# A running sum of squares: additions on GpSimd replaced by accumulating DMAs between SBUF tiles

## The chip, the core and the metric

One NeuronCore of a Trainium2 chip. The metric is the device time of one execution in microseconds; lower is better.

## The reference

The program computes two blocks on 512 tokens of 1024 features, in float32. The first is a recurrent layer (RG-LRU) with a layer norm, then a mixture of 32 experts with a second layer norm. The second block, where the change lies, has two layers, each of three parts with an RMS norm ahead of each, and an RMS norm at the very end:

```python
def rmsnorm(x, g):
    xf = x.astype(jnp.float32)
    y = xf * lax.rsqrt(jnp.mean(xf * xf, axis=-1, keepdims=True) + EPS)
    return (y * g.astype(jnp.float32)).astype(x.dtype)
...
    for l in range(DEPTH_2):
        h = rmsnorm(x, g_ffn1[l])
        x = x + 0.5 * swiglu(h, w1_a[l], w3_a[l], w2_a[l])
        h = rmsnorm(x, g_mix[l])
        p = h @ w_in[l]
        ...
        x = x + merged @ w_o[l]
        h = rmsnorm(x, g_ffn2[l])
        x = x + 0.5 * swiglu(h, w1_b[l], w3_b[l], w2_b[l])
    return rmsnorm(x, g_final)
```

So there are seven norms: three ahead of each layer's parts, twice, and the last one. The mixer in the middle of a layer has gates, a Fourier branch, a short convolution and a pooling branch; only its end and its place matter here.

## The kernel before

The dense stage keeps x transposed: `X[k]`, k = 0 to 7, holds features 128k to 128k + 127 on the partitions and all 512 tokens along the row, in float32. Weights stream in from DRAM in blocks of 1 MB; each half block (128 x 1024) is split into a high part `whi` (ScalarE, L135) and a low part `wlo` (VectorE, L136). Every product of a 128 x 128 weight tile is three matmuls of 128 x 512 (L172 to L174): high by high, high by low, low by high.

A norm needs, for each token, the sum of x squared over all 1024 features, that is over the partitions of eight tiles. The kernel adds up the squares tile by tile into `ssum` (128 x 512), and then sums over the partitions with TensorE: `rstd_1` multiplies pieces of `ssum` by a vector of ones (L1230), and VectorE and ScalarE make the factor 1/sqrt from it. The factor is not needed ahead of the next matmuls: those run on X times the gain (`xgh`, `xgl`, made by `prep`, L1218 and L1224), and their results are multiplied by the factor `R` afterwards.

How the pieces are laid in time:

- The second half of an FFN (`out_part`) goes through j = 0 to 7; for each j it sums ten products into one bank (30 matmuls), then `done(j)` adds the bank to `X[j]` on VectorE (L1342) and calls `nxt(j)`, which is `prep`: the high part on ScalarE, then `square(j)`, and the low part on VectorE.
- The second half of a mixer (`out_part2`) does the same with four products for each j, the fourth one three steps later. Towards its end only fourth products are left, so the last `done(j)` follow each other quickly (L1486).
- `square(k)` squares `X[k]` on ScalarE (L1208) into a buffer `t`, one of seven; for k = 0 it writes `ssum` itself. The addition of `t` to `ssum` (L1211) is put on a list, `late`, that is emitted after the next square by `flush`. Its engine is the argument `E`, GpSimd by default. Only the first of the seven norms passes VectorE (`squares`, called as `pre` of the first FFN).
- Behind the first two chunks of the next part (24 matmuls each) stands `rstd_1`, in TensorE's queue; in the very first FFN it is behind three. The engines take their instructions in the order in which they are emitted. Waits between engines, and those for DMAs, come from the tiles that instructions read and write.
- The last norm has its squares for k = 0 to 6 in `last`, which also scales the odd `X[k]` on GpSimd (L1495). The last tile, k = 7, is done by `tail` in two halves of 256 tokens, where `sums` (L1516) reads `ssum` and the squares of the last tile, with half of the second half's matmuls behind it.

GpSimd has, in the dense stage, these additions, L1495's scalings, some small memsets for the convolution's and the pooling's edges (L1355, L1356, L1424, L1425) and, at the very end, multiplications for the output (L1537). SyncE issues all weight loads.

Of the kernel before, what the change touches and what calls it, by code (L numbers as in the profile page):

```python
# [16 lines left out]
OP = mybir.AluOpType  # L17
# [12 lines left out]
CAP = 64  # L30
# [34 lines left out]


class Stream:
    """Weight blocks of 128 x 2048 in the order of use: DMA, then each half as hi + lo."""

    def __init__(self, tc, wpool, nr, nh):  # L70
        self.tc, self.nc = tc, tc.nc
# [9 lines left out]
        self.ns = 0  # L81

    def slots_from(self, pool, tag, n, lo=0, hi=1 << 30, bufs=None):
        """n more raw buffers, for blocks lo to hi"""
        new = [dict(pool=pool, tag=tag, bufs=bufs or n, blk=None, lo=lo, hi=hi) for _ in range(n)]
        self.slots += new
        return new

    def add(self, aps, keep=()):
        """keep: blocks that are not split but read as they come"""  # L90
        self.blocks += aps
        self.keep = set(keep)
        self.used = set()
# [44 lines left out]
        return True  # L138

    def split_first(self, i):  # L140
        """A piece of the first half"""
        a, b = FIRST[i]
        hi, lo = (t[:, a:b] for t in self.get(0))
        src = self.raw[0][:, a:b]
        self.nc.scalar.activation(hi, src, AF.Copy)
        self.nc.vector.tensor_tensor(lo, src, hi, op=OP.subtract)
# [5 lines left out]
        return self.half[h]  # L152

    def advance(self, h, defer=False):
        """Everything of half h (and before) has been emitted. defer: returns the low parts still to be emitted"""
        late = []
        self.used |= {b for b in self.keep if 2 * b + 1 <= h}
        while self.ns < min(2 * len(self.blocks), self.hold):
            ahead = sum(q // 2 not in self.keep for q in range(h + 1, self.ns + 1))
            if ahead > self.nh - 1 or self.ns // 2 >= self.nb + 1:  # L160
                break
            self._dma()
            if self.ns // 2 >= self.nb:
                break
            self._split(late if defer else None)
        self._dma()
        return late
# [120 lines left out]
def rec_phase(K):  # L288
# [253 lines left out]
        nc.gpsimd.tensor_tensor(x1l[c], zz[c], x1h[c], op=OP.subtract)  # L542

    PSW = {}
    # the first of two token tiles is ahead of the second at the end
    steps = [(k, i) for k in range(KR - 3) for i in range(2)]
    steps += [(KR - 3, 0), (KR - 2, 0), (KR - 3, 1), (KR - 1, 0), (KR - 2, 1), (KR - 1, 1)]

# [32 lines left out]
        nc.gpsimd.dma_start(t, A["ln1"][i:i + 1].to_broadcast([128, D]))  # L581
    for c in range(2, 4):
        PSW[c] = [bank() for _ in range(2)]
    # the first of the two further ahead
    steps = [(k, i) for k in range(4) for i in range(2)]
    steps += [(4, 0), (5, 0), (4, 1), (6, 0), (7, 0), (5, 1), (8, 0), (9, 0), (6, 1), (7, 1), (8, 1), (9, 1)]
    late = {1: [(ln_s, 0)], 3: [(ln_a, 1)], 5: [(ln_s, 1), (logits_t, 0), (ln_b, 0)],
# [37 lines left out]


def onehot(K, g, cs=range(4)):
    """One-hot rows of the slots of 4 experts: token on the partitions, slot on the columns"""
    nc, op, io = K["tc"].nc, K["op"], K["io"]
    V, P = nc.vector, nc.gpsimd if g else nc.vector  # L630
    if ("oh", g) not in K:
        K["oh", g] = (op.tile([128, 4, 4 * CAP], F32R, name="oh", tag="oh", bufs=2),
                      op.tile([128, 4, 2], F32, name="sg", tag="sg", bufs=2))
        P.tensor_scalar(K["oh", g][1], K["slot"], float(-4 * CAP * g), None, op0=OP.add)
    oh, sg = K["oh", g]
    for c in cs:
        if g and c < 3:
            for i in range(2):
                P.tensor_scalar(oh[:, c + i], io, sg[:, c, i:i + 1], None, op0=OP.is_equal)
            P.tensor_tensor(oh[:, c], oh[:, c], oh[:, c + 1], op=OP.add)  # L640
        else:
            V.tensor_scalar(oh[:, c], io, sg[:, c, 0:1], None, op0=OP.is_equal)
            V.scalar_tensor_tensor(oh[:, c], io, sg[:, c, 1:2], oh[:, c], op0=OP.is_equal, op1=OP.add)
# [66 lines left out]


def route_ids(K):
    """The ids of the tokens by expert"""
    pm, ohm = K["pm"], K["ohm"]
    P = K["tc"].nc.gpsimd
    bm = [128, 4, 2, NE]
    K["dd"] = K["gp"].tile([128, 4, NE], F32R, name="dd")
    P.tensor_tensor(pm, ohm, K["tid"][:, :, :, None].to_broadcast(bm), op=OP.mult)
    P.tensor_tensor(K["dd"], pm[:, :, 0], pm[:, :, 1], op=OP.add)
# [18 lines left out]
def moe_phase(K):  # L738
# [61 lines left out]
    HP, HS, YP = {}, {}, {}  # L800

    def mm_h(e, m, i):
        """Half of the features of the product of expert e with w1 or w3: columns 0:64 x high, 64:128 x low"""
        nonlocal h
        name = ("h1", "h3")[m]
        if i == 0:
            HP[m] = bank(name)
        ps = HP[m]
        for q in range(2):
            w = st.get(h)  # L810
            for r in range(2):
                k = 4 * i + 2 * q + r
                if e == 0 and m == 0:
                    if k == 0:
                        gather(0, 0)
                    if k + 1 < KD:
                        gather(0, k + 1)
                x = XT[e // 4][k][:, e % 4]
                sl = slice(r * 512, (r + 1) * 512)
                if k < KD - 1:  # L820
                    nc.tensor.matmul(ps, x, w[0][:, sl], start=k == 0, stop=False)  # L821
                nc.tensor.matmul(ps[:64], x[:, 0:64], w[1][:, sl], start=False, stop=False)  # L822
                if k == KD - 1:
                    nc.tensor.matmul(ps, x, w[0][:, sl], start=False, stop=True)  # L824
            if i and q:
                HS[m] = mp.tile([128, 512], F32, name=name + "s", tag=name + "s", bufs=1)
                act(HS[m], ps, AF.Copy)
            st.advance(h)
            h += 1
# [42 lines left out]
                in_=ysb, in_offset=None, bounds_check=2 * S - 1, oob_is_err=False)  # L872

    def place(c):
        """For the last two experts: gate by token and slot"""
        oh, sg = K["oh", NE // 4 - 1]
        if c == 0:
            K["og"] = (mp.tile([128, 4, 128], F32, name="og", tag="og", bufs=1), mp.tile([128, 128], F32, name="og1"))
        og, o1 = K["og"]
        for k, o in ((0, og[:, c]), (1, o1)):  # L880
            nc.gpsimd.tensor_scalar(o, io[:, 128:256], sg[:, c, k:k + 1], K["gt"][:, c, k:k + 1], op0=OP.is_equal, op1=OP.mult)
        nc.gpsimd.tensor_tensor(og[:, c], og[:, c], o1, op=OP.add)

    def place_t():
        """The same with the slot on the partitions"""
        P = mp.tile([128, 4, 128], F32, name="P", tag="P", bufs=1)
        pt = bank("ids")
        for c in range(4):
            nc.tensor.transpose(pt[:, c * 128:(c + 1) * 128], K["og"][0][:, c], ident)
        act(P, pt.rearrange("p (c t) -> p c t", c=4), AF.Copy)  # L890
        return P

    def overflow(nmax):
        """Slots beyond CAP of an expert, 64 at a time, for any routing."""
        NI = 16
        m7 = mp.tile([128, NE, 8], F32, name="ova", tag="og", bufs=1)
        xe = mp.tile([128, 2, NE], F32, name="xe")
# [169 lines left out]
        return [bank(*n) for n in ((("h1",), ("h3",)), (("y0",), ("y1",)), (("gat", 2), ("gat", 2)), (("ht",), ("ids",)))[c]]  # L1067

    def comb(c, *ab):
        """Sums of products into the two halves of z or of what has yet to be added to it"""  # L1070
        new = c not in PC
        if new:
            PC[c] = banks(c)
# [2 lines left out]
                nc.tensor.matmul(PC[c][i], a, b[:, i * 512:(i + 1) * 512], start=new and n == 0, stop=n == len(ab) - 1)  # L1076

    def stats(c):
        """z complete, its mean and variance"""
        m = mv[:, c]  # L1080
        for i in range(2):
            z = PC[c][i]
# [57 lines left out]


def both(f, g):
    """The steps of two sequences in turn"""
    f, g = iter(f), iter(g)
    go = True
    while go:
# [6 lines left out]


def newton(V, out, v, t):
    """The steps to out = 1/sqrt(v) from t = sqrt(v), one Newton step"""
    yield lambda: V.reciprocal(out, t)
    yield lambda: V.tensor_tensor(t, out, out, op=OP.mult)
    yield lambda: V.tensor_tensor(t, t, v, op=OP.mult)
# [4 lines left out]
def dense_phase(K):  # L1164
# [41 lines left out]
    def square(k, E=nc.gpsimd):  # L1206
        t = ssum if k == 0 else tmp()
        act(t, X[k], AF.Square)  # L1208
        flush()
        if k:  # L1210
            late.append(lambda: E.tensor_tensor(ssum, ssum, t, op=OP.add))  # L1211

    def prep(k, g, sq=True):
# [10 lines left out]
        late.insert(0, lambda: STT(lo, X[k], g(k), hi, op0=OP.mult, op1=OP.subtract))  # L1224

    def rstd_1():
        """rc = 1/sqrt(mean of squares + eps), a token on a partition"""
        pc = bank()
        for c in range(4):
            nc.tensor.matmul(pc[:, 2 * c:2 * c + 2], ssum[:, c * 128:(c + 1) * 128], onesf[:, 0:2],  # L1230
# [6 lines left out]
        TT(rc[:, 3], rc[:, 0], rc[:, 0], op=OP.mult)  # L1237

    def rstd_2(*out):
        """rc or its square, a token a column"""  # L1240
        for i in out:
            ps = bank()
            for c in range(4):
# [15 lines left out]
        return ps  # L1259

    def out_part(x, done, tail=None):
        """X[j] += x @ w for every j, the tiles of w in the order (j, k). tail: takes the last j instead"""
        nonlocal h
        n = 0
        for j in range(KD):
# [17 lines left out]
        h += n // 8  # L1283

    def out_part2(x, done):
        """The same for four x, the last one of them LAG2 j later"""
        nonlocal h
        ps = {}
        n = 0
# [19 lines left out]
    def ffn(nxt, pre=None, tail=None):  # L1309
        n = 0  # L1310

        def in_r():
            """A chunk, and behind an early one the steps to R"""
            nonlocal n
            ps = in_chunk()
            if n == 1 and pre:
# [178 lines left out]
            nc.gpsimd.tensor_scalar(X[k], X[k], vc("gfinal", k), None, op0=OP.mult)  # L1495

    def tail(x, w):
        """The last feature tile of X, the final norm and the output, half of the tokens ahead of the other half"""
        PX, PR = [bank() for _ in range(2)], {}
        sq = tmp()  # L1500

# [73 lines left out]


def layout(I):
    """The inputs as the program reads them: slices, transposes and zero padding only."""
    f = np.float32
    A = {}  # L1580
    x = np.asarray(I["x"])[0]
# [19 lines left out]
    A["ln1"] = np.ascontiguousarray(np.stack([np.asarray(I["ln_g"])[0, 0], np.asarray(I["ln_b"])[0, 0]]))  # L1601

    def tiles(w):
        """[K, N] -> [N/128, 128, K/128, 128]: for each chunk of outputs its stationary tiles."""
        K, N = w.shape
        return w.reshape(K // 128, 128, N // 128, 128).transpose(2, 1, 0, 3)

    blocks = []

    def put(a):  # L1610
        """[n, 128, 1024] halves"""
        a = np.asarray(a).reshape(-1, 128, HB)
        if len(a) % 2:
            a = np.concatenate([a, np.zeros((1, 128, HB), f)])
# [106 lines left out]
```

## Time and profile before

| | us |
|---|---|
| median of 2 runs | 3045.65 (3044.44 to 3046.87) |
| span of the profiled execution | 3045.3 |
| TensorE busy | 2972.5 (98%) |
| VectorE busy | 1743.2 (57%) |
| ScalarE busy | 1302.1 (43%) |
| GpSimd busy | 282.3 (9%) |

The profile is that of one execution of 3045.3 us from its first to its last instruction; the runs' median is 0.35 us above that. Shares are of the span. Matmuls overlap each other in TensorE, so that a busy share of 98% says that it hardly ever stands still, not that it is at its peak. The mean granted clock of TensorE is 0.991 of full speed.

### The profile page before, as it was taken

How to read it: one execution, taken by the hardware profiler on the slowest of the kernel's cores; microseconds unless marked ns; L12 is line 12 of the kernel's file. 1: busy time of each engine (PE TensorE's matmuls, PEld its weight loads, DVE VectorE, ACT ScalarE, POOL GpSimd, SP SyncE). 2: the span in 40 equal slices, each digit the busy share in tenths (PEclk: the TensorE clock that was granted, in tenths of full speed). 3: DMA queues.
4: the chain of work that ended last, by engine and by line, in shares of the span. 5: the costliest groups of instructions: out<-in, count | busy, mean ns of one | idle time of the engine just before them, and what ended most of it. 6: DMA issues, size and time to landing. Idle time of an engine off the chain costs nothing.

```text
span 3045.3 us, 33566 instructions
## 1 busy us (share of the span) xinstructions
PE 2972.5 (98%) x13360; PEld 2338.3 (77%) x13360; DVE 1743.2 (57%) x2127; ACT 1302.1 (43%) x1687; POOL 282.3 (9%) x235
## 2 busy tenths in 40 slices
PE   9997999999899999999999999999999999999998
PEld 7875666666568888888878888888888888878887
DVE  7678888898974344455555334443344465544343
ACT  4746888888753223233233223322223332332222
POOL 0025222220600000000010000100001000100002
PEclk9998999999999999999999999999999999999999
DMA  6374899999822222222222222222222222232221
GB/s 191 119 277 171 342 363 347 373 371 374 319 80 88 96 97 97 92 81 105 97 97 97 97 97 83 97 97 96 99 83 97 83 97 100 94 109 86 96 97 56
DMA packets 75360, 452.18 MB, mean 148 GB/s; under 512 B 8684, under 2 KB 19308, under 8 KB 22336
## 3 DMA queue, kind: packets, MB, share of 16 engines
q1 hardware_dynamic: 71040, 441.78, 39.4%
q0 software_dynamic: 3072, 7.17, 0.6%
q8 instruction: 106, 1.74, 0.2%
q10 hardware_dynamic: 1088, 1.05, 0.1%
q14 instruction: 54, 0.44, 0.0%
HBM read 439.79 MB, written 14.16 MB: 149 GB/s over the span
## 4 chain that ended last, share of the span: by engine, by line
PE 77%; DVE 4%; ACT 2%; issue 1%; POOL 0%; POOLq 0%; DVEq 0%; ACTq 0%
PE mm L172 23%; PE mm L173 23%; PE mm L174 23%; DVE wlo L136 2%; PE y L857 2%; PE h L822 2%; PE h L821 1%; ACT whi L135 1%; PE ht L835 1%; PE gat L792 1%; DVE xgl L1224 0%; DVE z L1064 0%; DVE X L1486 0%; PE h L824 0%; ACT X L1114 0%
## 5 line engine op out<-in xcount | busy, mean ns | idle before, releaser
L136 DVE TENSOR_TENSOR wlo<-raw,whi 128x1024 fp32r<-128x1024 f32 x533 | 663.9, 1255 | 432.3 <-ACT whi L135 432.3
L172 PE MATMUL mm<-xgh,whi 128*128 128x512 f32 x2048 | 810.6, 396 | 2.2 <-ACT xgh L1218 2.2
L173 PE MATMUL mm<-xgl,whi 128*128 128x512 f32 x2048 | 809.8, 395 | 2.1 <-DVE xgl L1224 2.1
L174 PE MATMUL mm<-xgh,wlo 128*128 128x512 f32 x2048 | 809.2, 395 | 0.0
L135 ACT ACTIVATE whi<-raw 128x1024 fp32r<-128x1024 f32 x535 | 557.9, 1052 | 498.3 <-PE mm L173 457.3
L173 PEld LDWEIGHTS mm<-xgl,whi 128*128 128x128 f32 x2048 | 386.1, 189 | 94.5 <-DVE xgl L1224 4.3
L172 PEld LDWEIGHTS mm<-xgh,whi 128*128 128x128 f32 x2048 | 386.2, 189 | 93.1 <-ACT xgh L1218 2.6
L174 PEld LDWEIGHTS mm<-xgh,wlo 128*128 128x128 f32 x2048 | 386.1, 189 | 90.7
L172 PE MATMUL mm<-s,whi 128*128 128x512 f32 (+1 forms) x938 | 368.0, 392 | 0.0
L173 PE MATMUL mm<-s,whi 128*128 128x512 f32 (+1 forms) x938 | 367.9, 392 | 0.0
L174 PE MATMUL mm<-s,wlo 128*128 128x512 f32 (+1 forms) x938 | 367.8, 392 | 0.0
L1187 ACT ACTIVATE s<-t 128x512 fp32r<-128x512 f32 x128 | 81.0, 633 | 376.2 <-DVE t L1337 298.8
L1211 POOL TENSOR_TENSOR ssum<-ssum,t 128x512 f32<-128x512 f32 x41 | 57.0, 1391 | 1740.2 <-ACT t L1208 1739.5
L136 DVE TENSOR_TENSOR wlo<-rawb,whi 128x1024 fp32r<-128x1024 f32 x162 | 203.6, 1298 | 22.7 <-ACT whi L135 20.6
L172 PEld LDWEIGHTS mm<-s,whi 128*128 128x128 f32 x938 | 176.6, 188 | 40.8
L173 PEld LDWEIGHTS mm<-s,whi 128*128 128x128 f32 x938 | 176.6, 188 | 40.8
L174 PEld LDWEIGHTS mm<-s,wlo 128*128 128x128 f32 x938 | 176.6, 188 | 40.6
L822 PE MATMUL h<-wlo,xt 128*64 128x512 f32 x512 | 195.6, 402 | 7.0 <-DVE wlo L136 6.3
L1336 DVE TENSOR_TENSOR t<-mm,R 128x512 f32<-128x512 f32 x88 | 60.8, 691 | 224.4 <-PE mm L174 224.4
L821 PE MATMUL h<-whi,xt 128*128 128x512 f32 x448 | 181.4, 405 | 5.9 <-PEq L1033 5.0
L1342 DVE SCALAR_TENSOR_TENSOR X<-mm,X 128x512 f32<-128x512 f32 x63 | 43.6, 692 | 227.8 <-PE mm L174 227.8
L857 PE MATMUL y<-whi,hd 128*64 128x512 f32 x512 | 161.6, 397 | 2.5 <-ACT whi L135 1.5
(356 smaller groups left out, 3281.7 us busy)
## 6 DMA issues: line engine op xcount, KB each, us to landing
raw<-in_wblocks SPq DMA_DIRECT2D x265, 1024.0 KB, 4.8
rawb<-in_wblocks SPq DMA_DIRECT2D x81, 1024.0 KB, 6.8
rawa<-in_wblocks SPq DMA_DIRECT2D x57, 1024.0 KB, 6.6
YD<-cs SPq DMA_DIRECT2D x8, 512.0 KB, 7.3
xt<-in_wblocks SPq DMA_DIRECT2D x4, 1024.0 KB, 8.3
rawb<-YD SPq DMA_DIRECT2D x3, 1024.0 KB, 4.8
z<-in_x POOLq DMA_DIRECT2D x4, 512.0 KB, 9.3
raw<-in_dfts SPq DMA_DIRECT2D x2, 1024.0 KB, 4.8
```

Source lines behind the costliest of these rows:

```text
L135: self.nc.scalar.activation(hi, src, AF.Copy)
L136: f = lambda E=self.nc.vector: E.tensor_tensor(lo, src, hi, op=OP.subtract)
L172: nc.tensor.matmul(ps, wh, xh, start=first, stop=False)
L173: nc.tensor.matmul(ps, wh, xl, start=False, stop=False)
L174: nc.tensor.matmul(ps, wl, xh, start=False, stop=last)
L821: nc.tensor.matmul(ps, x, w[0][:, sl], start=k == 0, stop=False)
L822: nc.tensor.matmul(ps[:64], x[:, 0:64], w[1][:, sl], start=False, stop=False)
L857: nc.tensor.matmul(ps[i][:64], hd[:, f, v:v + 64], w[wv][:, sl], start=f == 0 and n == 0, stop=f == 3 and n == 2)
L1187: act(hi, src, AF.Copy)
L1211: late.append(lambda: E.tensor_tensor(ssum, ssum, t, op=OP.add))
L1336: TT(v, p3, R, op=OP.mult)
L1342: STT(X[j], ps, 0.5, X[j], op0=OP.mult, op1=OP.add)
```

## The change

In `square`, an addition whose engine is GpSimd becomes a DMA issued from GpSimd, which adds the tile `t` to `ssum` as it writes (`accum_op`). The additions of the first norm, which pass VectorE, stay. The other lines of the diff take out docstrings and comments.

```diff
@@ -1207,7 +1207,9 @@
         t = ssum if k == 0 else tmp()
         act(t, X[k], AF.Square)
         flush()
-        if k:
+        if k and E is nc.gpsimd:
+            late.append(lambda: nc.gpsimd.dma_start(ssum, t, accum_op=OP.add))
+        elif k:
             late.append(lambda: E.tensor_tensor(ssum, ssum, t, op=OP.add))
```

## Rows read from the trace of the kernel before

**Rows 1.** The page, parts 1 and 4: busy time by engine; shares of the chain.

```profile
PE 2972.5 (98%) x13360; PEld 2338.3 (77%) x13360; DVE 1743.2 (57%) x2127; ACT 1302.1 (43%) x1687; POOL 282.3 (9%) x235
...
PE 77%; DVE 4%; ACT 2%; issue 1%; POOL 0%; POOLq 0%; DVEq 0%; ACTq 0%
```

**Rows 2.** Instructions of line L1211: count; ns min/median/max, first and last start.

```profile
L1211 POOL TENSOR_TENSOR ssum<-ssum,t x41: 1291/1306/1661, 1197.1 to 3026.3; 128x512 f32<-128x512 f32 x41
```

**Rows 3.** Timeline of GpSimd behind an FFN: start, duration, instruction, [idle before <-releaser].

```profile
1197.12 1.30 POOL L1211 TENSOR_TENSOR ssum<-ssum,t 128x512 f32<-128x512 f32 x1 [345.55 <-ACT t L1208]
...
1239.01 1.30 POOL L1211 TENSOR_TENSOR ssum<-ssum,t 128x512 f32<-128x512 f32 x1 [5.68 <-ACT t L1208]
```

**Rows 4.** Timeline of TensorE: the reads of the sum in three norms.

```profile
1247.84 0.95 PE L1230 MATMUL mm<-onesf,ssum 128*128 128x2 f32 x8
...
1590.46 0.95 PE L1230 MATMUL mm<-onesf,ssum 128*128 128x2 f32 x8
...
3029.91 0.28 PE L1516 MATMUL mm<-onesf,ssum 128*128 128x2 f32 x2
```

**Rows 5.** Timeline of GpSimd behind the first layer's mixer.

```profile
1570.80 1.29 POOL L1211 TENSOR_TENSOR ssum<-ssum,t 128x512 f32<-128x512 f32 x1 [144.34 <-ACT t L1208]
1572.35 1.45 POOL L1211 TENSOR_TENSOR ssum<-ssum,t 128x512 f32<-128x512 f32 x1 [0.26 <-ACT t L1208]
1576.90 8.50 POOL L1211 TENSOR_TENSOR ssum<-ssum,t 128x512 f32<-128x512 f32 x5 [3.11 <-ACT t L1208]
```

**Rows 6.** Timeline of GpSimd ahead of the last norm.

```profile
2991.20 1.31 POOL L1211 TENSOR_TENSOR ssum<-ssum,t 128x512 f32<-128x512 f32 x1 [324.40 <-ACT t L1208]
...
3026.27 1.30 POOL L1211 TENSOR_TENSOR ssum<-ssum,t 128x512 f32<-128x512 f32 x1 [4.16 <-ACT t L1208]
```

**Rows 7.** Timeline of VectorE behind the first layer's mixer: low parts of X.

```profile
1576.66 0.74 DVE L1224 SCALAR_TENSOR_TENSOR xgl<-X,vec,xgh 128x512 fp32r<-128x512 f32 x1
...
1577.92 1.19 DVE L1224 SCALAR_TENSOR_TENSOR xgl<-X,vec,xgh 128x512 fp32r<-128x512 f32 x1
```

**Rows 8.** Timeline of TensorE behind the first layer's mixer: its waits.

```profile
1582.60 0.50 PE L173 MATMUL mm<-xgl,whi 128*128 128x512 f32 x1 [0.30 <-DVE xgl L1224]
...
1584.30 0.50 PE L173 MATMUL mm<-xgl,whi 128*128 128x512 f32 x1 [0.75 <-DVE xgl L1224]
```

**Rows 9.** Timeline of ScalarE behind the first layer's mixer: squares.

```profile
1570.11 0.61 ACT L1208 ACTIVATE t<-X 128x512 f32<-128x512 f32 x1
...
1582.09 0.61 ACT L1208 ACTIVATE t<-X 128x512 f32<-128x512 f32 x1
```

**Rows 10.** DMA issues: queue, count, KB of each, median us to landing.

```profile
z<-in_x POOLq DMA_DIRECT2D x4, 512.0 KB, 9.3
...
outT<-X ACTq DMA_DIRECT2D x4, 256.0 KB, 2.3
...
g<-in_ln POOLq DMA_DIRECT2D x1, 512.0 KB, 4.6
...
YD<-ysb,idi POOLq DMA_INDIRECT x15, 8.2
...
cs<-in_dftc POOLq DMA_DIRECT2D x1, 128.0 KB, 3.5
```

**Rows 11.** Windows: stretch, length, busy by engine, TensorE's clock, DMA share, GB/s.

```profile
1580.00:1590.00 10.00, 8.95 (x38) 6.61 (x37) 8.75 (x7) 6.48 (x8) 5.16 (x4) 1.00 0.25 87
860.00:861.00 1.00, 0.80 (x4) 0.81 (x5) 1.00 (x4) 1.00 (x4) 0.00 (x0) 0.50 0.00 0
870.00:871.00 1.00, 1.00 (x6) 0.82 (x5) 1.00 (x2) 1.00 (x2) 0.00 (x0) 1.00 0.00 0
```

**Rows 12.** Timeline of TensorE: start of the dense stage; transposes of the last norm.

```profile
864.37 0.80 PE L172 MATMUL mm<-xgh,whi 128*128 128x512 f32 x1 [2.20 <-ACT xgh L1218]
...
870.00 0.40 PE L172 MATMUL mm<-xgh,whi 128*128 128x512 f32 x1
...
3032.57 0.38 PE L1529 MATMUL mm<-ident,rc 128*128 128x128 f32 x2
...
3037.54 0.69 PE L1529 MATMUL mm<-ident,rc 128*128 128x128 f32 x2 [3.01 <-DVE rc L1161]
```

## The prediction

> **What bounds the kernel now.** I read the page first. TensorE is busy 98% of the span and carries 77% of the chain that ended last; GpSimd carries 0% of that chain [rows 1]. So an edit that only takes work off GpSimd buys nothing by itself; it matters if it makes TensorE wait. Then I looked up the edited line: 41 additions of 1.306 us median [rows 2]. 41 is 7 + 7 + 7 + 7 + 7 + 6: six norms use the line on GpSimd; the first of the seven norms passes VectorE and keeps its additions. What matters is therefore not how busy the line is but how much time lies between the last square of each norm and the matmuls that read the sum. I took that from the timeline of GpSimd and the matmuls of L1230 and L1516.
>
> There are three kinds of norm.
> - Behind the second half of an FFN (three times) seven additions come 30 matmuls apart, from 1197.12 to 1239.01, one every 41.89/6 = 6.98 us [rows 3], and the sum is read at 1247.84 [rows 4]. From the start of the last addition to the read there are 8.83 us. The other two norms of this kind look alike.
> - Behind a mixer (twice) seven squares come in a burst: the first addition starts at 1570.80, the last five are back to back and end at 1585.40 [rows 5]. The sum is read at 1590.46 [rows 4], 19.66 us after the first addition started. The mixer of the second layer looks alike.
> - The last norm has six additions, 7 us apart, from 2991.20 to 3026.27 [rows 6], and TensorE reads the sum at 3029.91 [rows 4]: 3.64 us after the last addition started.
>
> In each case the read stands in TensorE's own queue, in order, with the next chunk of matmuls behind it. If the sum is late, TensorE stands still, and as it bounds the kernel there is no slack to pay from.
>
> **The change part by part.** It removes 41 x 1.306 = 53.5 us of GpSimd time, which hid beside TensorE: worth nothing directly. Indirectly it is worth a little: while additions run, VectorE's low parts (L1224) take 1.19 us where a free one takes 0.74 [rows 7], and behind a mixer TensorE then waits for them 0.30 + 0.75 = 1.05 us [rows 8]. Two mixers: at most 2.1 us to win, provided that nothing later makes TensorE wait anyway.
>
> It adds 41 DMAs of 256 KB from t into ssum. Each one reads and writes ssum, so each must wait until the one before has landed, and GpSimd, which issues them, must wait for that in its queue. The pieces thus form a chain. Call P the time of one link: issue to landing, plus some 0.1 us to wake the next issue (from a square's end, 1570.11 + 0.61, to the start of its addition it is 0.08 us [rows 5, 9]). The link was 1.3 us; P decides everything.
>
> No accumulating DMA is in this trace, so P is bounded by the nearest rows [rows 10]. From below: a 256 KB store of X out of SBUF lands 2.3 us after its issue, from ScalarE's queue. On GpSimd's queue: 128 KB take 3.5 us, 512 KB take 4.6 us, the scatter of an expert pair's results takes 8.2, and four 512 KB loads issued together 9.3. An accumulation of 256 KB has to fetch both t and ssum, 512 KB in all, so the row that I hold nearest is the one of 512 KB, 4.6 us, issued from GpSimd. Behind a mixer the DMA share is 0.25 [rows 11], so there is room. I take P = 4.6 + 0.1 = 4.7 us and keep 2.4 and 9.4 as ends.
>
> The Trainium skill bears on that choice. "Collectives: The Full Stack", section "The bandwidth ceiling", says that an addition inside the DMA engines is slower than a copy because it needs two source reads and not because the adding costs time; no run here shows it yet. With the constants of "DMA: Bandwidth & Descriptors", section "Anatomy of one DMA" (about 2.0 us fixed plus bytes at 436 GB/s), two reads would give an estimate of 3.2 us and a sum of some 3053 to 3058 us in place of mine.
>
> Mixers: the chain starts at 1570.80 as before and takes 7 x 4.7 = 32.9 us, since the squares all come sooner than the links end. The read is 32.9 - 19.66 = 13.2 us late. TensorE stands still for that and the 1.05 us that it used to wait earlier. Does its clock fall? In this trace TensorE, after idling 3.0 us ahead of the last transposes, has 0.69 us for a pair that took 0.38 [rows 12]; and before the dense stage, after gaps of 1 to 2 us, the granted clock is 0.50 (1.2 of 2.4 GHz) from 860 on and 1.00 again by 870 [rows 11]. Between 864.37 and 870.00 there start 12 matmuls [rows 12], which at the full clock take 12 x 6.98/30 = 2.8 us: 2.8 us lost. A stand-still of 14 us should see the same fall, so 13.2 + 2.8 = 16.0 us each, 32.0 for the two. The 1.05 us gain vanishes in this wait: with the chain late, an earlier arrival of TensorE only waits longer. Bounds for the clock term are 0 and 2.8 us.
>
> FFN norms: as long as P is below 6.98 no link waits for its predecessor, and the last one, issued at 1239.01, has 8.83 us. Three times nothing; the cover is the two chunks of matmuls between. Beyond P = 7.25 (1197.12 + 7P = 1247.84) it is gone.
>
> Last norm: 4.7 - 3.64 = 1.1 us late. Everything to the end hangs on it, so 1.1 us.
>
> GpSimd itself: its queue now stands still until the link before has landed. Behind it are only small memsets for the convolution, needed after the norm's factor, and L1495's scaling of X, needed only for the output. The time of the issues on GpSimd is inside P. The buffers t are seven; behind a mixer they now stay taken until the chain has read them, but the next user comes only after the norm's factor exists. VectorE and ScalarE wait behind the factor's first steps; the weight halves that the next chunks need were split ahead of that. All that costs nothing.
>
> Sum: 32.0 + 0 + 1.1 = 33.1 us. The profiled execution has a span of 3045.3 us, 0.35 below the median of 3045.65, so I add the sum to the median: 3078.8, say **3079 us** (+1.1%).
>
> In general, for P between 3.64 and 7, the sum is 2 x (7P - 19.66 + 2.8) + (P - 3.64) = 15P - 37.4 us. Each microsecond of P costs 15.
>
> **The rivals.**
> - *The chain fits.* If a link costs what the store from SBUF costs, 2.3 + 0.1 us, the chain behind a mixer is 16.8 us, less than 19.66 - 1.05, and 2.4 is less than 3.64 at the end. Nothing waits and the 2.1 us of VectorE's disturbance come back: 3043.5 us. For it: data that stay in SBUF, and a light DMA load. Against it: every row from GpSimd's queue is at 3.5 us or more. It decides below P = 2.8. Chance 0.10. The fit in "DMA: Bandwidth & Descriptors" (the Trainium skill, section as above), taken for 256 KB without a second read, gives an estimate of 2.6 us per transfer, with which the chain would just fit, some 3044 us; GpSimd's 128 KB row at 3.5 us speaks against it.
> - *The links do not wait, or nothing changes.* If the accumulations were issued without waiting for each other, only the last link would count: its square ends at 1582.09 + 0.61 = 1582.70 [rows 9], and 1582.70 + 4.7 = 1587.4 is ahead of the read at 1590.46, also with the 1.05 us taken off: some 3044 us. If the new branch were not taken (the engine compared is a default argument), the kernel would be the old one, 3045.7. Both unlikely, since each DMA writes the tile that the next reads. Chance 0.05 together.
> - *The link is slow, and the norms behind the FFNs go too.* From P = 6.55 the sum is over 60.9 us, which is 2%. A price from the trace is the scatter of the experts, the one DMA that GpSimd issues out of SBUF: 8.2 + 0.1. Then each mixer costs 58.1 - 19.66 + 2.8 = 41.2 us, each FFN norm ends at 1197.12 + 58.1 = 1255.2, that is 7.4 + 2.8 = 10.2 us late (three: 30.6), and the last norm's chain ends at 2991.20 + 6 x 8.3 = 3041.0, 11.1 us late. Sum 124 us: 3170 us, slower by 4%. For it: reading and writing the same tile in the DMA engines may be served at less than copy speed, and weight loads cut in. Against it: that row is a scatter by indices into DRAM, beside the experts' weight stream. Chance 0.23.
>
> **How the numbers follow.** Forecast (P from 2.8 to 6.55) 0.62, chain fits 0.10, no waiting or no change 0.05, slow link 0.23. The forecast's own range, for P from 3.5 to 6.5, is 3061 to 3106 us. The range that should hold 8 of 10 takes in the two cases near 3044 at its lower end and goes up to P = 7.3 (15 x 7.3 - 37.4 = 72 us): 3043 to 3118. Left out is mainly the upper part of the slow link, about 0.15. Slower by over 2%, which is about what a measurement of this kernel tells from no change, is the slow link alone, 0.23; faster by over 2% has no mechanism here, 0.01; the rest 0.76.
>
> **What the changed profile would show.** Behind each mixer: seven DMA issues on GpSimd, their starts P apart (4.7 us), and TensorE idle ahead of L1230 for 13 to 15 us, with the granted clock at 0.50 just behind it. Behind the FFNs: L1230 starts without idle time. At the end: about 1 us idle before L1516. VectorE's low parts back at 0.74 us. Wrong would be: issues closer than 2.8 us or not in a chain (no stand-still), idle time ahead of L1230 behind the FFNs (P above 7.25), or a stand-still without a fall of the clock, which takes 2.8 us off each mixer.

## The result and the profile after

The changed kernel takes 3078.86 us (median of 2, 3077.60 to 3080.11) against 3045.65 before: ratio 1.0106, interval 1.0077 to 1.0136. Run again beside the kernel before it took 3078.65 against 3048.61 us: ratio 1.0097 (1.0080 to 1.0114), 30 us. It is about 1% slower, as forecast (3079 us). The lines below are from the profiled execution of 3080.11 us, span 3078.3, against the span of 3045.3 before. Behind the edit the line numbers are two higher: the read of the sum is L1232 and L1518, the low parts of X are L1226.

First the page of the changed kernel, busy time and the chain:

```profile
PE 2981.9 (97%) x13360; PEld 2343.3 (76%) x13360; DVE 1726.4 (56%) x2127; ACT 1301.5 (42%) x1687; POOL 257.2 (8%) x235
...
PE 12%; POOL 0%; DMA 0%; issue 0%; POOLq 0%; ACT 0%; DVE 0%
```

The chain no longer covers the kernel as in [rows 1]: followed back from the end it comes through 12% of the span to a DMA, and stops there. In order of time that DMA is the first piece of the chain:

```profile
2696.99 3.31 DMA ssum<-t
```

It is the last accumulation behind the second mixer. So the chain says where to look. GpSimd is less busy than before (257.2 against 282.3 us) and the kernel is slower.

The timeline of GpSimd behind the first mixer, in place of [rows 5] (start, duration, instruction, idle time before it and what ended it):

```profile
1572.58 0.85 POOL L1211 DMA_DIRECT2D ssum<-t  x1 [144.55 <-ACT t L1208]
1576.99 0.85 POOL L1211 DMA_DIRECT2D ssum<-t  x1 [3.56 <-DMA ssum<-t]
1580.75 0.85 POOL L1211 DMA_DIRECT2D ssum<-t  x1 [2.91 <-ACT t L1208]
1584.52 0.85 POOL L1211 DMA_DIRECT2D ssum<-t  x1 [2.92 <-ACT whi L135]
1589.06 0.85 POOL L1211 DMA_DIRECT2D ssum<-t  x1 [3.69 <-DMA ssum<-t]
1595.98 0.85 POOL L1211 DMA_DIRECT2D ssum<-t  x1 [6.07 <-DMA ssum<-t]
1599.80 0.85 POOL L1211 DMA_DIRECT2D ssum<-t  x1 [2.97 <-DMA ssum<-t]
```

The issues are 4.41, 3.76, 3.77, 4.54, 6.92 and 3.82 us apart. Where the releaser is given as a ScalarE instruction, all squares up to that one had been there for a while; what really ended the wait was the DMA before. TensorE on the same stretch, for [rows 4], with the matmuls that follow:

```profile
1590.19 0.40 PE L174 MATMUL mm<-xgh,wlo 128*128 128x512 f32 x1
1603.11 1.86 PE L1232 MATMUL mm<-onesf,ssum 128*128 128x2 f32 x8 [12.52 <-DMA ssum<-t]
1604.84 0.77 PE L172 MATMUL mm<-xgh,whi 128*128 128x512 f32 x1
...
1611.05 0.39 PE L172 MATMUL mm<-xgh,whi 128*128 128x512 f32 x1
```

From the first issue to the read it is 30.53 us; TensorE stood still for 12.52 us. The windows of this stretch show its clock (length, busy time by engine, then the granted clock, DMA share, GB/s):

```profile
1588.00:1590.00 2.00, 2.00 (x11) 1.61 (x10) 0.00 (x0) 0.00 (x0) 0.85 (x1) 1.00 1.07 451
...
1592.00:1594.00 2.00, 0.00 (x0) 0.00 (x0) 0.00 (x0) 0.00 (x0) 0.00 (x0) 0.89 0.95 264
1594.00:1596.00 2.00, 0.00 (x0) 0.00 (x0) 0.00 (x0) 0.00 (x0) 0.02 (x1) 0.50 0.47 84
...
1608.00:1610.00 2.00, 2.00 (x6) 1.61 (x5) 0.00 (x0) 0.00 (x0) 0.00 (x0) 0.50 0.00 0
1610.00:1612.00 2.00, 2.00 (x9) 1.53 (x9) 0.00 (x0) 0.00 (x0) 0.00 (x0) 0.85 0.00 0
```

At the start two weight loads are under way together with the accumulations, with a DMA share of 1.07. In the kernel before they stand at the same place, without accumulations beside them:

```profile
1588.00:1590.00 2.00, 2.00 (x11) 1.59 (x10) 0.75 (x1) 0.00 (x0) 0.00 (x0) 1.00 0.97 381
```

The changed kernel's clock falls to 0.50 (1.2 of 2.4 GHz) during the wait and is back at 1.00 only around 1610.5, over 7 us after work began again. From the start of the read to the sixteenth matmul after it, 1603.11 to 1611.05, it takes 7.94 us; before, the same stretch took 4.38 us (1590.46 to 1594.84). So the fall costs 3.56 us. Behind the second mixer it costs less. The lines of the kernel before (the sixteenth matmul of the first mixer, then the read and the sixteenth matmul of the second) and of the changed kernel (the second mixer):

```profile
1594.84 0.40 PE L172 MATMUL mm<-xgh,whi 128*128 128x512 f32 x1
...
2671.86 0.95 PE L1230 MATMUL mm<-onesf,ssum 128*128 128x2 f32 x8
...
2676.25 0.39 PE L172 MATMUL mm<-xgh,whi 128*128 128x512 f32 x1
```

```profile
2700.35 1.87 PE L1232 MATMUL mm<-onesf,ssum 128*128 128x2 f32 x8 [12.24 <-DMA ssum<-t]
...
2707.57 0.40 PE L172 MATMUL mm<-xgh,whi 128*128 128x512 f32 x1
```

That is 7.22 us in place of 4.39: 2.83 us.

The other norms: the timeline of TensorE behind an FFN and at the end.

```profile
1249.50 0.95 PE L1232 MATMUL mm<-onesf,ssum 128*128 128x2 f32 x8
...
3061.24 0.28 PE L1518 MATMUL mm<-onesf,ssum 128*128 128x2 f32 x2
```

Neither has a wait in front of it. The waits of TensorE in all say the same (who waits for whom: us in total, times, longest):

```profile
PE mm L1232 <- DMA ssum<-t: 24.8, 2, 12.5
```

and the summary of the tile `ssum` gives the time from an issue to its landing:

```profile
DMA to landing us min/median/max: 3.2/3.3/6.4
```

One more place differs, and it lies at the very end. Each engine's part of the program closes with an instruction named DRAIN (L1716 before, L1718 after), in which GpSimd stays for some microseconds. It has three; the longest is the first. Before:

```profile
L1716 POOLq DRAIN  x3: 46/109/4017, 3038.7 to 3045.0; - x3
```

After:

```profile
L1718 POOLq DRAIN  x3: 46/109/7367, 3070.1 to 3078.0; - x3
```

Before, it lasts 4.0 us and is done 2.6 us ahead of the program's end; in the changed kernel it lasts 7.4 us and is done 0.8 us ahead of it. From the read of the last norm to the end it takes 15.4 us before (3029.91 to 3045.3) and 17.1 us after (3061.24 to 3078.3), 1.7 us more. The length of this wait goes with the number of DMAs that GpSimd has issued in the whole program: 4.02 us with 22, 5.16 with 36 (e2 below), 6.22 with 49 (e1) and 7.37 with 63, which is 0.08 us for each.

The sum of the traces: 24.8 us of waiting at two reads, plus 3.56 + 2.83 = 6.4 us for the clock, less what the low parts gave back. The row of L1226 now has a largest duration of 754 ns, before it was 1810, and the 2.1 us of TensorE's waits for them are gone. Counted by the starts of the matmuls it is 1.4 us behind each mixer: a matmul ahead of the first burst starts at 1560.75 before and 1562.31 after, 1.56 us later, but TensorE reaches the read at 1603.11 - 12.52 = 1590.59 against 1590.46, only 0.13 us later. So 24.8 + 6.4 - 2.9 = 28.3 us for the two mixers, and with the 1.7 us at the end 30.0 us, which is also what the repeated comparison gives. The spans of the two first traces differ by 33.0. Of the other 3 us, about half lie ahead of the first mixer and the rest in the first FFN of the second layer, where 30 matmuls take 7.00 us in place of 6.97; e5, with the same 41 DMAs, has 6.97 there, so I give this remainder no cause.

### The profile page after: what moved, and what is told of

Same layout as the page of the kernel before. It is cut to its first block, busy times and chain, and to the rows that moved or that the text cites. A ratio compares the mean times of both kernels' runs of the same rounds, so it can differ in the third digit from the quotient of the medians.

```text
span 3078.3 us, 33592 instructions
## 1 busy us (share of the span) xinstructions
PE 2981.9 (97%) x13360; PEld 2343.3 (76%) x13360; DVE 1726.4 (56%) x2127; ACT 1301.5 (42%) x1687; POOL 257.2 (8%) x235
## 5 line engine op out<-in xcount | busy, mean ns | idle before, releaser
L136 DVE TENSOR_TENSOR wlo<-raw,whi 128x1024 fp32r<-128x1024 f32 x533 | 654.0, 1237 | 442.6 <-ACT whi L135 442.5
L1211 POOL DMA_DIRECT2D ssum<-t x41 | 35.0, 855 | 1793.8 <-ACT t L1208 1755.8
L135 ACT ACTIVATE whi<-rawb 128x1024 fp32r<-128x1024 f32 x162 | 163.4, 1055 | 0.1
```

The costliest lines, as they stand in the source:

```text
L136: f = lambda E=self.nc.vector: E.tensor_tensor(lo, src, hi, op=OP.subtract)
L1211: late.append(lambda: nc.gpsimd.dma_start(ssum, t, accum_op=OP.add))
```

## The experiments

Theory A is that of the prediction: behind a mixer, the seven accumulations wait for one another, the sum comes late, and TensorE waits and loses its clock; everything else is hidden. Its first rival, B, is that each DMA costs something wherever it is.

**Only one kind of norm.** In e1 the two norms behind the mixers add on GpSimd, in e2 only they use DMAs. `mix` is true where the gain is that of the part behind a mixer.

```diff
-        if k and E is nc.gpsimd:
+        if k and E is nc.gpsimd and not mix:     # e1;  e2: and mix
             late.append(lambda: nc.gpsimd.dma_start(ssum, t, accum_op=OP.add))
```

> The two norms behind the mixers add on GpSimd again; the other four keep their 27 accumulating DMAs. Theory A (the serial chain of seven behind a mixer makes TensorE wait, everything else is hidden): 3045 to 3047 us, no wait at L1232. Theory B (each DMA costs something wherever it is, 33 us / 41 = 0.8 us each, through its traffic or its work on GpSimd): 27 x 0.8 = 22 us, 3067 us.

> The complement: DMAs only behind the two mixers (14 of 41). Theory A: the whole loss, 3077 to 3080 us, TensorE idle 12 us ahead of each L1232. Theory B: 14 x 0.8 = 11 us, 3057 us.

Measured: e1 3048.25 us against 3048.30 before, ratio 1.0002 (0.9992 to 1.0012); e2 3075.02 us, ratio 1.0091 (1.0075 to 1.0108), with 24.4 us of waits at L1232. 27 of the 41 DMAs cost nothing that the times show, and the other 14 carry 27 of the 30 us; e2 itself came out 2 us under the range expected for it. As an account of the loss B falls. What is left of it is the closing wait on GpSimd: from the last norm's read to the end e1 takes 15.9 us, 0.5 more than the kernel before.

**A shorter chain.** In e3 the odd tiles behind a mixer go to a second sum; the square of tile 1 is written into it directly, and L1232's matmuls read both.

```diff
+        a = ssum2 if mix and k % 2 else ssum
+        t = a if k == 0 or mix and k == 1 else tmp()
...
-            late.append(lambda: nc.gpsimd.dma_start(ssum, t, accum_op=OP.add))
+            late.append(lambda: nc.gpsimd.dma_start(a, t, accum_op=OP.add))
```

> Behind the mixers the even tiles accumulate into one sum and the odd ones into a second, so that two chains of three DMAs run side by side in place of one of seven (the matmuls with ones read both). 39 DMAs are left. Theory A (what costs is waiting for the link before): three links of 3.8 us from the third square on, about 1578 + 3 x 3.8 = 1589.5, land about when TensorE arrives at 1590.6: at most 3 us of waiting each, 3044 to 3052 us. Theory B (the DMAs themselves cost): 39/41 of the loss, 3077 us.

Measured: 3066.51 us, ratio 1.0063 (1.0047 to 1.0080). This lies between the two expectations and fits neither. The timeline of TensorE (of the fastest of the four executions, 3062.97 us) shows both waits shorter, 5.38 and 2.62 us in place of 12.52 and 12.24, and neither gone:

```profile
1597.07 3.15 PE L1237 MATMUL mm<-onesf,ssum 128*128 128x2 f32 x14 [5.38 <-DMA ssum<-t]
...
2683.60 1.72 PE L1237 MATMUL mm<-onesf,ssum 128*128 128x2 f32 x14 [2.62 <-DMA ssum<-t]
```

The longest landing here is 10.2 us. The last accumulation was issued at 1586.87 and landed just ahead of 1597.07. SyncE had issued two 1 MB weight loads at 1586.3 and 1588.6, and they too took longer, 7.8 and 9.4 us; in e1, where no DMA of the sum is beside them, the same two took 4.8 and 5.5. In the changed kernel the two long links, the fourth and the fifth DMA of the chain (4.54 and 6.92 us to the next issue; the text ahead of e8 counts them, by the issue that comes late, as five and six), fall on the same two loads (issued at 1585.37 and 1587.64, DMA share 1.07 above). The first link, 4.41 us, falls on a single load issued at 1570.43. That is a second cause that the prediction had priced at nothing, tried further below.

**Reading later.** In e4 all DMAs stay; the read in the FFN behind a mixer stands three chunks further back.

```diff
-            if n == (2 if pre else 1):
+            if n == (2 if pre else 4 if two else 1):
                 rstd_1()
-            if n == (3 if pre else 2):
+            if n == (3 if pre else 5 if two else 2):
...
-                if f == 0:
+                if f == 0 or two and f == 1:
                     continue
```

> All 41 DMAs as in the change, but in the FFN behind a mixer the matmuls that read the sum stand three chunks later (16.7 us of matmuls between). Theory A: the chain's 12.5 us are covered, TensorE does not stand still and its clock does not fall: 3043 to 3047 us. Theory B (the cost is not that wait): 3079 us as the change.

Measured: 3046.88 us, ratio 0.9996 (0.9986 to 1.0005). With the same 41 DMAs the loss is gone; TensorE does not wait for the sum, and its clock is 1.00 in the windows from 1588 to 1604. The long links are still there (4.50 and 7.25 us between issues). So it is the wait at the read that costs, not the chain as such. It does not beat the kernel before by more than a trifle, 1.4 us, inside the interval: the low parts give back 2.9 us, and the closing wait takes 1.4 of them (16.8 us from the last norm's read to the end against 15.4).

**The clock by itself.** e5 fills the wait with matmuls that nothing uses.

```diff
+        for _ in range(54 * two):
+            nc.tensor.matmul(pc, XG[0][0][:, 0:128], XG[0][0], start=True, stop=True)
         for c in range(4):
             nc.tensor.matmul(pc[:, 2 * c:2 * c + 2], ssum[:, c * 128:(c + 1) * 128], onesf[:, 0:2],
```

> The change, with 54 matmuls of 128x512 into the bank of the norm's factor ahead of the reads behind a mixer (12.6 us at the full clock; their result is overwritten and used by nothing). They fill the time in which TensorE waits. Theory A (the fall of the clock is a cost of its own, 3.6 us each): the granted clock stays at 1.00 and 7 us are won, 3072 us. Theory C (the wait alone costs, the clock is made good elsewhere): 3079 us.

Measured: 3071.69 us against 3049.04, ratio 1.0076 (1.0059 to 1.0093), where the change has 1.0097 (1.0080 to 1.0114): some 6 us won. The intervals overlap, and the two were not measured beside the same executions of the kernel before; but all four executions of e5 (3069.09 to 3074.12) lie under all four of the change (3077.83 to 3079.60). The spans of the two profiles differ by 7.6 us (3069.9 and 3077.5). In its windows the clock holds:

```profile
1592.00:1600.00 8.00, 8.00 (x37) 6.64 (x36) 0.00 (x0) 0.00 (x0) 1.70 (x2) 1.00 0.42 72
1600.00:1604.00 4.00, 3.77 (x21) 2.95 (x20) 1.73 (x8) 1.15 (x2) 0.00 (x0) 1.00 0.06 9
```

TensorE now waits 0.2 us at each read. So theory A's second half holds: the fall of the clock is a cost of its own, and work without any use takes it away. The 6 us agree with the 3.56 + 2.83 us of the traces better than with twice 3.6.

**What a link is made of.** e6 copies in place of accumulating, so that the sum is left with the last square copied; e7 accumulates half of the columns and leaves out the others.

```diff
-            late.append(lambda: nc.gpsimd.dma_start(ssum, t, accum_op=OP.add))
+            late.append(lambda: nc.gpsimd.dma_start(ssum, t))                                                        # e6
+            late.append(lambda: nc.gpsimd.dma_start(ssum[:, 0:S // 2], t[:, 0:S // 2], accum_op=OP.add))             # e7
```

> The same chain of DMAs, but each one copies t over ssum and adds nothing (six of the eight squares of a norm and more are left out of the sum). The difference is the price of accumulating. Theory D (an accumulation must fetch 512 KB; the rows of 128 KB at 3.5 us and 512 KB at 4.6 us give 0.7 us for the second 256 KB): links 0.7 us shorter, 14 of them, 10 us less: 3069 us. Theory E (a link is latency, not bytes): 3079 us, landing still 3.3 us.

> The same accumulating chain, but only 256 of the 512 tokens (128 KB of 256 KB in each DMA; the squares of the other tokens are left out of the sum, but for the first tile's). Theory D (bytes): links shorter by 0.7 us or more, 3069 us or less. Theory E (latency): landing 3.0 to 3.3 us, 3077 to 3079 us; only the two links that meet a weight load could become shorter.

Measured: e6 3066.50 us, ratio 1.0057 (1.0040 to 1.0074); e7 3071.51 us, ratio 1.0071 (1.0051 to 1.0091). The summaries of `ssum` in the two traces, e6 first:

```profile
L1211 POOL DMA_DIRECT2D ssum<-t x41: 536/536/657, 1196.4 to 3043.9; - x41
...
DMA to landing us min/median/max: 2.2/2.3/6.2
```

```profile
L1211 POOL DMA_DIRECT2D ssum<-t x41: 837/849/994, 1197.6 to 3049.5; - x41
...
DMA to landing us min/median/max: 2.6/2.7/7.9
```

An accumulation of 256 KB lands after 3.3 us, a copy of the same size after 2.3, an accumulation of 128 KB after 2.7. Theory E (latency alone) falls. D holds for e6, with 1.0 us instead of 0.7 for accumulating; e7 misses D's numbers, with links 0.6 us shorter (3.2 us between issues) instead of 0.7 or more and 3071.5 us instead of 3069 or less. The issue on GpSimd is longer too, 0.85 against 0.54 us. The rest shows in the queue of GpSimd's DMAs (packets, MB, share of 16 engines' span), e6 ahead of the changed kernel:

```profile
q0 software_dynamic: 6352, 17.92, 1.6%
```

```profile
q0 software_dynamic: 8976, 17.92, 2.7%
```

Before, without the 41, it was 0.6%. So accumulating takes 2.1% x 3078.3/41 = 1.6 us of all 16 engines for each DMA, copying 1.0% x 3064.6/41 = 0.75 us: twice as much for the same 256 KB (the shares are given to 0.1%, so these are good to some 0.1 us). e7 gained less in its time than in its landings, since in its trace the link that meets the weight loads is longer, 8.43 us between issues.

**The weight loads.** e8 holds the two loads back: a small DMA on SyncE's queue reads the sum and stands ahead of them. e9 is e3 with the same, for both sums.

```diff
         flush()
+        if hold:
+            nc.sync.dma_start(scr, ssum[:, 0:8])
         st.advance(h + 3)
```

> The change itself, unaltered, beside the next two on the same chip. All theories: 1.009 to 1.013 of the kernel before, 3077 to 3084 us.

> The change, with the two 1 MB weight loads that follow a mixer held back on SyncE's queue until the sum has landed (a small DMA that reads the sum stands ahead of them). Theory F (links five and six are long, 4.5 to 6.9 us, because those loads take the same DMA engines): all links 3.8 to 4.4 us, the two waits shorter by 3.9 and 3.5 us, 7 us less than the change: 3072 us. Theory G (a link of the chain is long for another reason, such as its place or the idle engines): the same as the change. Should the loads be missed, TensorE would wait for weights behind the norm: slower than the change.

> Two sums of three links each, as before, and the two weight loads held back until both have landed. Theory F: two short chains with free DMA engines land before or about when TensorE arrives: no wait over 2 us at the reads, no fall of the clock, 3047 to 3053 us. Theory G: as with two sums alone, +15 to +18 us on the kernel before.

Measured: the change again 3078.65 us, ratio 1.0097; e8 3070.88 us, ratio 1.0073 (1.0056 to 1.0090); e9 3048.81 us, ratio 1.0000 (0.9991 to 1.0010). GpSimd's timeline in e8:

```profile
1582.98 0.85 POOL L1212 DMA_DIRECT2D ssum<-t  x1 [2.91 <-DMA ssum<-t]
1586.82 0.85 POOL L1212 DMA_DIRECT2D ssum<-t  x1 [2.99 <-DMA ssum<-t]
1590.63 0.85 POOL L1212 DMA_DIRECT2D ssum<-t  x1 [2.97 <-DMA ssum<-t]
1594.41 0.85 POOL L1212 DMA_DIRECT2D ssum<-t  x1 [2.93 <-DMA ssum<-t]
```

These links are 3.8 us again (the first, under the load that was not held back, is still 4.54), and the two waits add up to 17.2 us instead of 24.6 in the change's second profile: 7.4 us, as expected. The times agree: all four executions of e8 (3069.32 to 3071.62) lie under all four of the change. In e9 nothing waits behind the mixers; its two reads (16 matmuls now) follow at once on the chunk ahead:

```profile
1592.47 0.39 PE L174 MATMUL mm<-xgh,wlo 128*128 128x512 f32 x1
1592.70 1.84 PE L1239 MATMUL mm<-onesf,ssum 128*128 128x2 f32 x16
```

Theory F holds. The miss of e3 is then explained: two short chains would have been in time, and the weight loads made them late. One thing stays open: in e3 and e9 the very last read waits 1.4 and 1.2 us for its accumulation, although nothing was edited there and no weight load is under way. With a margin of 3.5 to 3.6 us there and a landing of 3.3 a little is enough; these two accumulations land after 5.1 and 4.8 us. While e9's is under way, one packet of another queue moves on the DMA engines, the queue that the view calls instruction:

```profile
q0 software_dynamic: 144, 0.26, 31.1%
q8 instruction: 1, 0.02, 1.9%
```

e3 has the same beside its last accumulation, and the changed kernel, which lands there after 3.3 us, has no such packet. So the packet may be the cause; this is not shown, since no run moves it away.

## Why the prediction was right, step by step

- *What bounds it, and where the cost arises:* right, and shown by e1 and e2 (mixers alone) and e4 (the read, not the DMAs).
- *The chain of seven:* predicted 7 x 4.7 = 32.9 us, measured 30.53. The size is nearly right and its make-up is not. P was taken as 4.6 us of landing and 0.1 of waking. Landing is 3.3 us; the row of 512 KB was too dear a neighbour, and the same list had a second one, `b<-in_ln` at 7.8 us, that the prediction did not name. From a landing to the next issue it is some 0.5 us (issues 3.8 us apart), not 0.1: the 0.08 us of [rows 5, 9] is a wake by a ScalarE instruction, and did not carry over to a DMA. And "so there is room", read from a DMA share of 0.25 over 10 us [rows 11], was wrong: the mean hides that the loads come as 2 MB at a stretch at the end of that window, with a share of 0.97 already in the kernel before. These two loads add 3 to 4 us to each chain (e8). The seven landings are 3.9, 3.2, 3.2, 4.0, 6.4, 3.3 and 3.3 us, 27.3 in all. So landing alone was too high by 1.3 x 7 = 9.1 us, waking too low by 2.5 (3.2 us for six wakes, 0.7 predicted) and the loads were left out with 4.2: that nets to the 2.4 us by which the chain was over. That these errors cancel is luck.
- *Waiting net of the low parts:* predicted 13.2 us for each mixer, measured (24.8 - 2.9)/2 = 11.0. The low parts did go back to 0.74 us and their waits vanished, as was said, into the longer one.
- *The clock:* predicted 2.8 us each, measured 3.56 and 2.83; it falls as foreseen, and e5 shows that it costs.
- *FFN norms:* nothing, as predicted.
- *Last norm:* predicted 1.1 us, measured 0: 3.3 us of landing fit into the 3.5 us between the last issue (3057.75) and the read (3061.24).
- *GpSimd itself:* predicted to cost nothing. Its queue showed no cost, but the closing wait that grows with its DMAs was not thought of: 1.7 us at the end of the program.
- *Sum:* 33.1 us predicted; 33.2 measured in the first comparison, of two executions each, and 30.0 in the larger one. The single number, 3079 us, came out closer than its terms deserve: the mechanism was right, and the hit to the microsecond is luck.
- *Rivals:* the chain fits (P below 2.8) is refuted by links of 3.8 us, though a plain copy of 2.3 us, 2.8 us between issues, comes near to it: e6 still waits 12.2 us in two places. The links do wait for each other. The slow link is refuted; links of 6 to 7 us exist, but only under the weight loads.
- *The Trainium skill:* its page "Collectives: The Full Stack", section "The bandwidth ceiling", holds the second read to be the cost of adding in the DMA engines. The doubled engine time (1.6 against 0.75 us) and the 1.0 us between e6 and the change agree with that; that the adding itself is free no run here separates. The fit on the Trainium skill's page "DMA: Bandwidth & Descriptors", section "Anatomy of one DMA", gave an estimate of 3.2 us with two reads, and 3.3 was measured; for 256 KB with one read it gave an estimate of 2.6, and the copy of e6 took 2.3. As a link of a chain the estimate was short by the 0.5 us of waking and by the weight loads, so its sum of 3053 to 3058 us was too low.

## What to carry to other kernels

Here, giving a step to a DMA turned an addition of 1.3 us into a link of 3.8 us or more. Where such steps depend on each other, count the links between the last input and the reader, not the busy time of the engine that is relieved. A reader that stands later in the queue took the cost away (e4), and so did two shorter chains together with loads that are held back (e9), but only back to the time before. Price a link at the moment at which it runs: ask which bulk loads are issued just then, since a mean DMA share does not show them. And a wait on the bounding engine can cost more than its length: here 2.8 to 3.6 us more for a wait of 12, because TensorE's clock came back late.

## What the runs showed of the hardware that was not expected

- Accumulating is not a copy with a flag: 0.85 against 0.54 us to issue on GpSimd, 3.3 against 2.3 us to land and 1.6 against 0.75 us of all DMA engines, for 256 KB inside SBUF.
- A small transfer under a bulk load paid about two to three times its price: 3.3 us alone, 6.4 us under two 1 MB loads, and 10.2 us in e3, where another accumulation was under way for part of it (what of this is due to that one was not tried); the loads themselves went from 4.8 and 5.5 us (e1) to 7.8 and 9.4 (e3).
- Each DMA that GpSimd issues made its closing wait 0.08 us longer, from 4.0 us with 22 of them to 7.4 with 63, accumulations, plain copies (e6) and half-width ones (e7) alike.
